# One hybrid decoder layer: transposed products gathered in one half bank of PSUM, with their evacuation and the SSD inputs' products on VectorE

## The chip, the cores and the metric

The kernel runs on one core of one Trainium2 chip. The metric is the device time of one execution in microseconds (us), lower is better. The median of three runs of the kernel before is 1099.75 us.

## The reference, cut to what matters

One decoder layer on 256 rows of width 2048, in float32. A combined input projection feeds a Mamba-2 SSD head group and a sparse-attention head group with its token indexer; one output projection maps both into the residual, and a squared-ReLU MLP of width 8192 follows.

```python
h = rmsnorm(x, g_mix) @ w_in
z, xbc, dt, q, k, v, qi, ki, wi = _split(h, IN_SIZES)
xbc = jax.nn.silu(causal_dwconv(xbc, conv_w, conv_b))
xs, bm, cm = _split(xbc, (SSD_WIDTH, N_BC, N_BC))
...
y = ssd_chunked(xs_f, dt_f, a, ...)          # uses xs * dt
y = y + d_skip.astype(jnp.float32)[:, None] * xs_f
...
y_att = dsa_attention(q, k, v, qi, ki, wi)   # scores from relu(qi . ki), top 64 keys
x = x + jnp.concatenate([y_ssd, y_att], axis=-1) @ w_out
u = rmsnorm(x, g_mlp) @ w_up
return x + jnp.square(jax.nn.relu(u)) @ w_down
```

## The kernel before, in words

Each matrix product is done with weights and activations split into a high and a low part, and three terms are summed: high by high, low by high, high by low. `operands` loads a weight tile on SP's queue (L122), ScalarE casts out the high part (L125) and VectorE subtracts it to get the low part (L126). It has 4 buffers for the raw tile (`raw`) and 5 for the split one (`w2`), and the splits are given high priority, so that they run ahead of TensorE.

There are two kinds of product. `product` has rows on partitions and sums all three terms in one whole bank for each of two row blocks (L148 to L150). `product_t` has columns on partitions: it makes 256 output columns by 256 rows from four weight tiles, with matmuls that stream 256 columns (L200). It is used for 4 blocks of the indexer's queries (`qi`), 6 blocks of the convolution's channels (`xbc`) and the 32 blocks of `w_up`, 42 in all. Before, it holds two banks, one for each 128 output columns; in each, the high by high term goes to the first half bank and the other two terms to the second half. `total` then adds the halves: ScalarE copies one half out of PSUM (L209), VectorE adds the other (L210).

The order of TensorE's instructions is that of the program. Small tasks (convolution, scores, top-k, SSD, attention) are Python generators; `step` advances them between groups of matmuls, so that their transposes and small matmuls are spread over the big products. The order on the other engines is set ahead of time by a planner from priorities and its own costs, and does not change when the chip runs.

For each `xbc` block, `conv` evacuates the product into `xraw` (L209, L210), GpSimd multiplies it by the rows' norm factors into `pad` (L510), ScalarE and VectorE do the four taps (L514, L516), and ScalarE the SiLU (L518). Blocks 0 to 3 are transposed by TensorE (L524), and ScalarE copies the result from PSUM to `xs` (L525). When the third block's task is done, `inputs` multiplies on GpSimd: `xs` by `dt` into `xdt` (in `room`, L535, two halves), `xdt` by the state's decay into `xdd` (L537), and `xs` by the skip weight in place (L540, two halves). Blocks 4 and 5 are the `bc` tile. The block `m1` of the input projection (608 columns in two K tiles, L148 to L150 with 304 columns) follows the `xbc` blocks in TensorE's order; inside it stand the small matmuls `ps_cb` (L550), which wait for `bc`. Beside them VectorE sums the indexer's scores (`sc`, L480) and takes the top 64 keys (L488, L489).

In the MLP, `up` evacuates each `w_up` product with `total`, squares its positive part on VectorE (L797), and splits the result again (L799, L800); `down` multiplies by `w_down`.

Of the kernel before, what the change touches and what calls it, by code (L numbers as in the profile page):

```python
# [9 lines left out]
F32 = mybir.dt.float32  # L10
F32R = mybir.dt.float32r
I32 = mybir.dt.int32
AF = mybir.ActivationFunctionType
OP = mybir.AluOpType
AX = mybir.AxisListType

P = 128
D = 2048
T = 256
NB = T // P  # L20
KT = D // P
# [47 lines left out]
def hymba_kernel(ctx: ExitStack, tc: tile.TileContext, xn, xt, w_in, w_out, w_up, w_down, vcol, vrow, out):  # L69
    nc = tc.nc  # L70
# [4 lines left out]
    ps = ctx.enter_context(tc.tile_pool(name="ps", bufs=4, space=bass.MemoryType.PSUM))  # L75
    mid_stack = ExitStack()
    mid = mid_stack.enter_context(tc.tile_pool(name="mid", bufs=1))

    u4 = dict(tag="u4", bufs=6)
    u2 = dict(tag="u2", bufs=6)  # L80
# [28 lines left out]
    def vcp(name, i=0):  # L109
        return vc[:, VC[name] + i:VC[name] + i + 1]  # L110
# [20 lines left out]
    def mp(name):  # L131
        other.append(name)
        return ps.tile([P, 512], F32, name=name, tag="mid")

    def accumulators():
        return [ps.tile([P, 512], F32, name="acc", tag="acc") for _ in range(2)]

    def product(src, n, left, load=None, tail=None):


        acc = accumulators()
        last = KT if tail is None else KT - 4

        def part(kt, out, b, wh, wl):
            s = slice(b * P, (b + 1) * P)
            ah, al = left(kt)
            free = tail is not None
            nc.tensor.matmul(out, ah[:, s], wh, start=(kt == 0), stop=False, skip_group_check=free)  # L148
            nc.tensor.matmul(out, al[:, s], wh, start=False, stop=False, skip_group_check=free)  # L149
            nc.tensor.matmul(out, ah[:, s], wl, start=False, stop=(kt == KT - 1), skip_group_check=free)  # L150

        kept = []
        halves = [slice(0, n // 2), slice(n // 2, n)]
        if tail is not None:
            acc.append(mp("acc_t"))
        for kt in range(KT):
            if kt % 2 == 0:
                hi, lo = operands(src[kt // 2], 2 * n, load, 0 if tail is None else SPARE - SHIFT_T)
            w = slice(kt % 2 * n, kt % 2 * n + n)
            wh, wl = hi[:, w], lo[:, w]  # L160
            if tail is None:
                for b in range(NB):
                    part(kt, acc[b][:, :n], b, wh, wl)
            elif kt < last:
                for c in halves if kt else [slice(0, n)]:
                    part(kt, acc[0][:, c], 0, wh[:, c], wl[:, c])
                for i, c in enumerate(halves):
                    part(kt, acc[1 + i][:, c], 1, wh[:, c], wl[:, c])
            else:
                kept.append((kt, wh, wl))  # L170
            step()
        if tail is not None:
            for kt, wh, wl in kept:
                for c in halves:
                    part(kt, acc[0][:, c], 0, wh[:, c], wl[:, c])
            tail(0, slice(0, n), acc[0])
            for i, c in enumerate(halves):
                for kt, wh, wl in kept:
                    part(kt, acc[1 + i][:, c], 1, wh[:, c], wl[:, c])
                tail(1, c, acc[1 + i][:, c])  # L180
        other.append("product")
        return acc

    def product_t(src, right):

        acc = accumulators()
        for i in range(4):
            hi, lo = operands(src[i], 1024, shift=SHIFT_T)
            c = i % 2
            for k in range(8):  # L190
                kt = 8 * (i // 2) + k
                x = right(kt)
                s = slice(k * P, (k + 1) * P)
                todo = [(hi, 0, 0, T), (lo, T, 0, T), (hi, T, T, T)]

                if other:
                    other.clear()
                    todo[:1] = [(hi, 0, 0, P), (hi, P, P, T - P)]
                for j, (w, at, fr, n) in enumerate(todo):
                    nc.tensor.matmul(acc[c][:, at:at + n], w[:, s], x[:, fr:fr + n], start=(kt + j == 0),  # L200
                                     stop=(kt == KT - 1 and j == len(todo) - 1), skip_group_check=True)
                if k % 4 == 3:
                    step()
        return acc

    def total(dst, acc):

        for c in range(2):
            nc.scalar.copy(dst[:, c, :], acc[c][:, T:])  # L209
            nc.vector.tensor_tensor(dst[:, c, :], acc[c][:, :T], dst[:, c, :], op=OP.add)  # L210


    ones = keep.tile([P, P], F32, name="ones")
# [3 lines left out]
    pt = ps.tile([P, 512], F32, name="ps_w", tag="mid")  # L217
# [40 lines left out]
    for name, cols in IN_BLOCKS:  # L258
        n = sum(b - a for a, b in cols)
# [47 lines left out]
    rrow = mid.tile([P, T], F32, name="rrow")  # L307
# [22 lines left out]
    xdt = room[:, :2048].rearrange("p (c x) -> p c x", c=NB)  # L330
# [73 lines left out]

    def index_queries(acc):

        t = mid.tile([P, 2, T], F32, name="qi", **u2)
        total(t, acc)
        st = mid.tile([P, 4, T], F32R, name="qis", **u4)
        qis.append(st)  # L410
        s4 = st.rearrange("p (c r) t -> p c r t", r=2)
        for i in range(2):
            s, o = slice(64 * i, 64 * i + 64), slice(64 - 64 * i, 128 - 64 * i)
            nc.scalar.copy(s4[s, :, i, :], t[s])
            nc.vector.tensor_tensor(s4[o, :, i, :], t[s], s4[s, :, i, :].bitcast(F32), op=OP.subtract)


    def row(n, w=16):
        return vr[:, VR[n]:VR[n] + w]

    dt = mid.tile([P, NB, 16], F32, name="dt")
# [3 lines left out]
    dst_ = mid.tile([P, 16], F32, name="dstate")  # L425
# [75 lines left out]
    xs = mid.tile([P, NB, 1024], F32, name="xs")  # L501
    bc = mid.tile([P, 4, T], F32, name="bc")
    hd = lambda t: t.rearrange("p (h d) -> p h d", d=64)

    def conv(acc, i):
        raw = mid.tile([P, 2, T], F32, name="xraw", **u2)
        total(raw, acc)
        pad = mid.tile([P, 2, T + 3], F32, name="pad", tag="pad", bufs=2)
        nc.gpsimd.memset(pad[:, :, :3], 0.0)
        nc.gpsimd.tensor_tensor(pad[:, :, 3:], raw, rrow[:, None, :].to_broadcast([P, 2, T]), op=OP.mult)  # L510
        o = mid.tile([P, 2, T], F32, name="xc", **u2) if i < 4 else bc[:, 2 * (i - 4):2 * (i - 4) + 2, :]
        for j in range(2):
            ct = 2 * i + j
            nc.scalar.activation(o[:, j, :], pad[:, j, 0:T], AF.Copy, scale=vcp("conv_w", ct))  # L514
            for k in range(1, 4):
                nc.vector.scalar_tensor_tensor(o[:, j, :], pad[:, j, k:k + T], vcp("conv_w", 12 * k + ct), o[:, j, :],  # L516
                                               op0=OP.mult, op1=OP.add)
            nc.scalar.activation(o[:, j, :], o[:, j, :], AF.Silu, bias=vcp("conv_b", ct))  # L518
        if i < 4:
            yield Y["conv"]  # L520
            pt = mp("ps_xs")
            for c in range(NB):
                for j in range(2):
                    nc.tensor.transpose(pt[:, (2 * c + j) * P:(2 * c + j + 1) * P], o[:, j, c * P:(c + 1) * P], ident)  # L524
            nc.scalar.copy(xs[:, :, 256 * i:256 * i + 256], pt.rearrange("p (c x) -> p c x", c=NB))  # L525

    xdd = [None]
    bn = mid.tile([P, T], F32, name="bn")
# [1 line left out]

    def inputs():
        yield "conv3"
        for c in range(NB):
            x3 = hd(xs[:, c, :])
            nc.gpsimd.tensor_tensor(hd(xdt[:, c, :]), x3, dt[:, c, :, None].to_broadcast([P, 16, 64]), op=OP.mult)  # L535
        xdd[0] = mid.tile([P, 1024], F32, name="xdd", **u4)
        nc.gpsimd.tensor_tensor(hd(xdd[0]), hd(xdt[:, 0, :]), dst_[:, :, None].to_broadcast([P, 16, 64]), op=OP.mult)  # L537
        for c in range(NB):
            x3 = hd(xs[:, c, :])
            nc.gpsimd.tensor_tensor(x3, x3, row("d_skip")[:, :, None].to_broadcast([P, 16, 64]), op=OP.mult)  # L540

    def states():
        yield "conv5"
# [233 lines left out]
    first = product_t(w_up[0], x2)  # L777
# [13 lines left out]
    def up(q):  # L791
        uh = mlp.tile([P, KT, T], F32R, name="uh")
        ul = mlp.tile([P, KT, T], F32R, name="ul")
        for j in range(8):
            r = mlp.tile([P, 2, T], F32, name="r")
            total(r, first if q + j == 0 else product_t(w_up[8 * q + j], x2))
            nc.vector.scalar_tensor_tensor(r, r, 0.0, r, op0=OP.max, op1=OP.mult)  # L797
            s = slice(2 * j, 2 * j + 2)
            nc.scalar.copy(uh[:, s, :], r)  # L799
            nc.vector.tensor_tensor(ul[:, s, :], r, uh[:, s, :].bitcast(F32), op=OP.subtract)  # L800
        return uh, ul
# [72 lines left out]
```

## Time and profile before

| | |
|---|---|
| median of 3 runs | 1099.75 us (1098.17 to 1099.8) |
| the profiled execution: time, span from the first to the last instruction | 1098.6 us, 1096.5 us |
| TensorE matmul busy | 1086.4 us, 99% of the span |
| TensorE weight load busy | 987.4 us, 90% |
| VectorE busy | 689.8 us, 63% |
| ScalarE busy | 534.5 us, 49% |
| GpSimd busy | 42.0 us, 4% |
| mean granted TensorE clock | 1.000 |

The time is about 2 us above the span, for what lies around the first and the last instruction. Shares of busy time are means over stages with different limits; matmuls are pipelined, and their ends are modelled, so that a busy TensorE can still be short of its pace.

### The profile page before, as it was taken

The numbers are of one execution on the slowest core, as the hardware profiler recorded it, in microseconds if no ns is written. First come the engines' busy times: TensorE is split into PE (matmuls) and PEld (weight loads), VectorE is DVE, ScalarE is ACT, GpSimd is POOL, SyncE is SP. The second block draws the span as 40 slices with busy tenths as digits, with TensorE's granted clock in tenths as the row PEclk, the third lists the DMA queues.
The fourth block names the chain that finished last, engine by engine and source line by source line (L and its number), as shares of the span: only waits on it lengthen the run. The fifth ranks groups of instructions, "written<-read, shape, count | busy, mean of one in ns | idle before, by whom it ended". The sixth has DMA issues, their size and how long they took to land.

```text
span 1096.5 us, 17759 instructions
## 1 busy us (share of the span) xinstructions
PE 1086.4 (99%) x7098; PEld 987.4 (90%) x7098; DVE 689.8 (63%) x976; ACT 534.5 (49%) x749; POOL 42.0 (4%) x41
## 2 busy tenths in 40 slices
PE   9999998999999999999999999999999999999998
PEld 7999997888888899999998889998889999888888
DVE  6776999677765666666665456665555665554443
ACT  7755555555765554444443334444334444333331
POOL 0010031122000000000000000000000000000000
PEclk9999999999999999999999999999999999999999
DMA  9856434643475556666566666665665666565662
GB/s 312 275 200 191 141 122 156 213 155 118 132 245 181 188 176 195 196 194 197 191 197 193 192 192 192 194 194 192 194 196 192 196 196 193 194 192 192 212 211 78
DMA packets 63746, 207.54 MB, mean 189 GB/s; under 512 B 7216, under 2 KB 11568, under 8 KB 63664
## 3 DMA queue, kind: packets, MB, share of 16 engines
q1 hardware_dynamic: 63520, 206.36, 58.8%
q8 instruction: 56, 0.92, 0.4%
q14 instruction: 26, 0.21, 0.1%
q10 hardware_dynamic: 144, 0.05, 0.0%
HBM read 204.29 MB, written 2.10 MB: 188 GB/s over the span
## 4 chain that ended last, share of the span: by engine, by line
PE 92%; DVE 3%; DMA 2%; issue 1%; ACT 1%; SPq 0%; ACTq 0%; DVEq 0%
PE acc L200 40%; PE acc L148 16%; PE acc L150 16%; PE acc L149 16%; DMA raw<-in_w_in 2%; DVE w L126 1%; DVE bc L516 1%; PE ps_y L587 1%; DMA xrow<-in_xn 1%; PE ps_sr L671 0%; PE ps_l L625 0%; PE ps_o L650 0%; ACT w L125 0%; PE ps_dec L578 0%; DVE sc L480 0%
## 5 line engine op out<-in xcount | busy, mean ns | idle before, releaser
L126 DVE TENSOR_TENSOR w<-raw,w 128x1024 fp32r<-128x1024 f32 (+3 forms) x400 | 468.5, 1174 | 374.1 <-ACT w L125 373.6
L125 ACT CAST w<-raw 128x1024 fp32r<-128x1024 f32 (+3 forms) x400 | 399.7, 1003 | 478.4 <-PE acc L150 255.5
L200 PE MATMUL acc<-x2x,w 128*128 128x256 f32 (+1 forms) x3077 | 349.8, 276 | 0.0
L200 PEld LDWEIGHTS acc<-x2x,w 128*128 128x128 f32 x3077 | 349.4, 188 | 0.2
L148 PE MATMUL acc<-w,uh 128*128 128x512 f32 (+1 forms) x527 | 199.9, 379 | 0.0
L149 PE MATMUL acc<-w,ul 128*128 128x512 f32 (+1 forms) x527 | 199.8, 379 | 0.0
L150 PE MATMUL acc<-w,uh 128*128 128x512 f32 (+1 forms) x527 | 199.8, 379 | 0.0
L150 PEld LDWEIGHTS acc<-w,uh 128*128 128x128 f32 x527 | 98.9, 188 | 18.8
L148 PEld LDWEIGHTS acc<-w,uh 128*128 128x128 f32 x527 | 98.9, 188 | 18.7
L149 PEld LDWEIGHTS acc<-w,ul 128*128 128x128 f32 x527 | 98.9, 188 | 18.7
L200 PE MATMUL acc<-hx,w 128*128 128x256 f32 (+1 forms) x978 | 114.9, 277 | 0.0
L200 PEld LDWEIGHTS acc<-hx,w 128*128 128x128 f32 x978 | 112.7, 188 | 0.0
L150 PE MATMUL acc<-w,hx 128*128 128x512 f32 (+1 forms) x224 | 82.6, 369 | 4.2 <-DVE w L126 4.1
L148 PE MATMUL acc<-w,hx 128*128 128x512 f32 (+1 forms) x224 | 85.0, 379 | 0.1
L149 PE MATMUL acc<-w,hx 128*128 128x512 f32 (+1 forms) x224 | 81.8, 365 | 0.0
L150 PEld LDWEIGHTS acc<-w,hx 128*128 128x128 f32 x224 | 42.0, 188 | 12.3 <-DVE w L126 5.8
L148 PEld LDWEIGHTS acc<-w,hx 128*128 128x128 f32 x224 | 42.2, 189 | 7.1 <-ACT w L125 0.8
L149 PEld LDWEIGHTS acc<-w,hx 128*128 128x128 f32 x224 | 42.1, 188 | 6.9 <-issue 0.7
L808 DVE SCALAR_TENSOR_TENSOR xr<-acc,rs,xr 128x512 f32<-128x512 f32 (+1 forms) x32 | 22.3, 735 | 9.2 <-PE acc L150 9.2
L210 DVE TENSOR_TENSOR r<-acc,r 128x256 f32<-128x256 f32 x64 | 26.8, 418 | 0.0
L148 PE MATMUL acc<-w,yah 128*128 128x512 f32 x64 | 25.7, 402 | 0.0
L148 PE MATMUL acc<-w,ysh 128*128 128x512 f32 x64 | 25.1, 392 | 0.0
(220 smaller groups left out, 726.7 us busy)
## 6 DMA issues: line engine op xcount, KB each, us to landing
raw<-in_w_up SPq DMA_DIRECT2D x128, 512.0 KB, 4.3
raw<-in_w_down SPq DMA_DIRECT2D x128, 512.0 KB, 4.4
raw<-in_w_in SPq DMA_DIRECT2D x72, 512.0 KB, 3.6
raw<-in_w_out SPq DMA_DIRECT2D x32, 512.0 KB, 3.5
raw<-in_w_in SPq DMA_DIRECT2D x16, 256.0 KB, 4.5
raw<-in_w_in SPq DMA_DIRECT2D x16, 152.0 KB, 5.3
raw<-in_w_in SPq DMA_DIRECT2D x8, 304.0 KB, 2.9
xT<-in_xt SPq DMA_DIRECT2D x16, 128.0 KB, 4.4
```

Source lines behind the costliest of these rows:

```text
L125: nc.scalar.copy(hi[:, s], raw[:, s])
L126: nc.vector.tensor_tensor(lo[:, s], raw[:, s], hi[:, s].bitcast(F32), op=OP.subtract)
L148: nc.tensor.matmul(out, ah[:, s], wh, start=(kt == 0), stop=False, skip_group_check=free)
L149: nc.tensor.matmul(out, al[:, s], wh, start=False, stop=False, skip_group_check=free)
L150: nc.tensor.matmul(out, ah[:, s], wl, start=False, stop=(kt == KT - 1), skip_group_check=free)
L200: nc.tensor.matmul(acc[c][:, at:at + n], w[:, s], x[:, fr:fr + n], start=(kt + j == 0), stop=(kt == KT - 1 and j == len(todo) - 1), skip_g ...
L210: nc.vector.tensor_tensor(dst[:, c, :], acc[c][:, :T], dst[:, c, :], op=OP.add)
L516: nc.vector.scalar_tensor_tensor(o[:, j, :], pad[:, j, k:k + T], vcp("conv_w", 12 * k + ct), o[:, j, :], op0=OP.mult, op1=OP.add)
L587: nc.tensor.matmul(pt[:, 64 * i:64 * i + 64], m[i // 4][:, i % 4, :], xdt[:, c, 64 * h:64 * h + 64], start=True, stop=True)
L808: nc.vector.scalar_tensor_tensor(xr[:, b, c], acc, rs4[:, b:b + 1], xr[:, b, c], op0=OP.mult, op1=OP.add)
```

## The change

`product_t` holds one bank in place of two: each 128 output columns have one half bank, in which all three terms are summed. `total` is gone. The consumers read the product from PSUM themselves: `index_queries` with the casts and subtractions that it had; `conv` with the multiplication into `pad`, which moves from GpSimd to VectorE; `up` with a ReLU on ScalarE and a multiplication by the product on VectorE. After the transposes in `conv`, VectorE multiplies the result from PSUM by the skip weight into `xs` and by `dt` into `xdt`, block by block, in place of ScalarE's copy and GpSimd's four multiplications over whole rows; `xdd` moves from GpSimd to VectorE.

```diff
-    def accumulators():
-        return [ps.tile([P, 512], F32, name="acc", tag="acc") for _ in range(2)]
+    def accumulator():
+        return ps.tile([P, 512], F32, name="acc", tag="acc")
     def product(src, n, left, load=None, tail=None):
-        acc = accumulators()
+        acc = [accumulator(), accumulator()]
     def product_t(src, right):
-        acc = accumulators()
+        acc = accumulator().rearrange("p (c t) -> p c t", c=2)
...
-                todo = [(hi, 0, 0, T), (lo, T, 0, T), (hi, T, T, T)]
+                todo = [(hi, 0, 0, T), (lo, 0, 0, T), (hi, 0, T, T)]
...
-                    nc.tensor.matmul(acc[c][:, at:at + n], w[:, s], x[:, fr:fr + n], start=(kt + j == 0),
-                                     stop=(kt == KT - 1 and j == len(todo) - 1), skip_group_check=True)
+                    nc.tensor.matmul(acc[:, c, at:at + n], w[:, s], x[:, fr:fr + n], start=(i + k + j == 0),
+                                     stop=(i >= 2 and k == 7 and j == len(todo) - 1), skip_group_check=True)
-    def total(dst, acc):
-        for c in range(2):
-            nc.scalar.copy(dst[:, c, :], acc[c][:, T:])
-            nc.vector.tensor_tensor(dst[:, c, :], acc[c][:, :T], dst[:, c, :], op=OP.add)
     def index_queries(acc):
-        t = mid.tile([P, 2, T], F32, name="qi", **u2)
-        total(t, acc)
...
-            nc.scalar.copy(s4[s, :, i, :], t[s])
-            nc.vector.tensor_tensor(s4[o, :, i, :], t[s], s4[s, :, i, :].bitcast(F32), op=OP.subtract)
+            nc.scalar.copy(s4[s, :, i, :], acc[s])
+            nc.vector.tensor_tensor(s4[o, :, i, :], acc[s], s4[s, :, i, :].bitcast(F32), op=OP.subtract)
     def conv(acc, i):
-        raw = mid.tile([P, 2, T], F32, name="xraw", **u2)
-        total(raw, acc)
...
-        nc.gpsimd.tensor_tensor(pad[:, :, 3:], raw, rrow[:, None, :].to_broadcast([P, 2, T]), op=OP.mult)
+        nc.vector.tensor_tensor(pad[:, :, 3:], acc, rrow[:, None, :].to_broadcast([P, 2, T]), op=OP.mult)
...
-            nc.scalar.copy(xs[:, :, 256 * i:256 * i + 256], pt.rearrange("p (c x) -> p c x", c=NB))
+            x4 = pt.rearrange("p (c h d) -> p c h d", c=NB, d=64)
+            for dst, f in ((xs, row("d_skip")[:, None, 4 * i:4 * i + 4, None]), (xdt, dt[:, :, 4 * i:4 * i + 4, None])):
+                nc.vector.tensor_tensor(dst[:, :, 256 * i:256 * i + 256].rearrange("p c (h d) -> p c h d", d=64), x4,
+                                        f.to_broadcast([P, NB, 4, 64]), op=OP.mult)
     def inputs():
         yield "conv3"
-        for c in range(NB):
-            x3 = hd(xs[:, c, :])
-            nc.gpsimd.tensor_tensor(hd(xdt[:, c, :]), x3, dt[:, c, :, None].to_broadcast([P, 16, 64]), op=OP.mult)
         xdd[0] = mid.tile([P, 1024], F32, name="xdd", **u4)
-        nc.gpsimd.tensor_tensor(hd(xdd[0]), hd(xdt[:, 0, :]), dst_[:, :, None].to_broadcast([P, 16, 64]), op=OP.mult)
-        for c in range(NB):
-            x3 = hd(xs[:, c, :])
-            nc.gpsimd.tensor_tensor(x3, x3, row("d_skip")[:, :, None].to_broadcast([P, 16, 64]), op=OP.mult)
+        nc.vector.tensor_tensor(hd(xdd[0]), hd(xdt[:, 0, :]), dst_[:, :, None].to_broadcast([P, 16, 64]), op=OP.mult)
     def up(q):
-            total(r, first if q + j == 0 else product_t(w_up[8 * q + j], x2))
-            nc.vector.scalar_tensor_tensor(r, r, 0.0, r, op0=OP.max, op1=OP.mult)
+            acc = first if q + j == 0 else product_t(w_up[8 * q + j], x2)
+            nc.scalar.activation(r, acc, AF.Relu)
+            nc.vector.tensor_tensor(r, r, acc, op=OP.mult)
```

## Rows read from the trace of the kernel before

**Rows 1.** The page's busy time: us, share of the span, instructions.

```profile
PE 1086.4 (99%) x7098; PEld 987.4 (90%) x7098; DVE 689.8 (63%) x976; ACT 534.5 (49%) x749; POOL 42.0 (4%) x41
```

**Rows 2.** The page's chain that ended last, shares of the span by engine.

```profile
PE 92%; DVE 3%; DMA 2%; issue 1%; ACT 1%; SPq 0%; ACTq 0%; DVEq 0%
```

**Rows 3.** Busy us (x instructions) by stretch: PE, PEld, DVE, ACT, POOL; PEclk, DMA, GB/s.

```profile
118.00:157.00 39.00, 39.00 (x344) 39.00 (x344) 36.67 (x77) 24.54 (x42) 5.51 (x7) 1.00 0.48 148
157.00:170.00 13.00, 13.00 (x109) 12.97 (x109) 11.80 (x11) 4.22 (x10) 10.94 (x5) 1.00 0.10 25
170.00:184.00 14.00, 9.37 (x61) 8.25 (x60) 13.55 (x35) 5.84 (x11) 1.29 (x1) 1.00 0.52 155
...
400.00:1093.00 693.00, 692.97 (x4671) 636.44 (x4668) 393.35 (x418) 298.44 (x349) 0.00 (x0) 1.00 0.60 191
```

**Rows 4.** Timeline of PE, block m1: start, us, instruction [idle before <- releaser].

```profile
165.75 0.30 PE L148 MATMUL acc<-w,hx 128*128 128x304 f32 x1
...
170.97 0.30 PE L149 MATMUL acc<-w,hx 128*128 128x304 f32 x1
...
174.01 0.41 PE L150 MATMUL acc<-w,hx 128*128 128x304 f32 x1 [2.74 <-DVE w L126]
...
176.88 0.41 PE L150 MATMUL acc<-w,hx 128*128 128x304 f32 x1 [0.93 <-DVE w L126]
...
183.58 0.94 PE L550 MATMUL ps_cb<-bc 128*128 128x128 f32 x6 [0.54 <-ACT bc L518]
...
186.25 0.39 PE L148 MATMUL acc<-w,hx 128*128 128x512 f32 x1
```

**Rows 5.** Timeline of POOL, 132 to 169 us.

```profile
132.59 1.29 POOL L510 TENSOR_TENSOR pad<-xraw,rrow 128x512 f32<-128x512 f32 x1 [7.75 <-DVE xraw L210]
...
157.68 4.80 POOL L535 TENSOR_TENSOR room<-xs,dt 128x1024 f32<-128x1024 f32 x2 [2.09 <-ACT xs L525]
162.44 2.08 POOL L537 TENSOR_TENSOR xdd<-room,dstate 128x1024 f32<-128x1024 f32 x1
164.49 4.13 POOL L540 TENSOR_TENSOR xs<-xs,vr 128x1024 f32<-128x1024 f32 x2
```

**Rows 6.** Timeline of DVE, 132 to 169 us.

```profile
132.63 2.33 DVE L126 TENSOR_TENSOR w<-raw,w 128x1024 fp32r<-128x1024 f32 x1
...
157.09 0.88 DVE L516 SCALAR_TENSOR_TENSOR bc<-pad,vc,bc 128x256 f32<-128x256 f32 x2
...
158.59 4.17 DVE L516 SCALAR_TENSOR_TENSOR bc<-pad,vc,bc 128x256 f32<-128x256 f32 x2
162.68 2.12 DVE L480 SCALAR_TENSOR_TENSOR sc<-rl,wis,sc 128x256 f32<-128x256 f32 x1
164.73 2.12 DVE L516 SCALAR_TENSOR_TENSOR bc<-pad,vc,bc 128x256 f32<-128x256 f32 x1
168.02 1.25 DVE L126 TENSOR_TENSOR w<-raw,w 128x608 fp32r<-128x608 f32 x1 [1.17 <-ACT w L125]
```

**Rows 7.** Timeline of ACT, the last SiLU of block 4.

```profile
166.89 0.51 ACT L518 ACTIVATE bc<-bc,vc 128x256 f32<-128x256 f32 x1 [5.63 <-DVE bc L516]
```

**Rows 8.** Groups by line and shape on DVE: count, busy us, mean ns, idle before.

```profile
L210 DVE TENSOR_TENSOR xraw<-acc,xraw 128x256 f32<-128x256 f32 x12 | 5.0, 416 | 0.0
...
L691 DVE TENSOR_TENSOR xs<-xs,zs 128x512 f32<-128x512 f32 x4 | 2.7, 684 | 0.8 <-ACT zs L687 0.8
...
L635 DVE TENSOR_TENSOR L<-L,sm 128x1024 f32<-128x1024 f32 x2 | 2.4, 1220 | 0.0
...
L595 DVE TENSOR_TENSOR yo<-ps_yo,eac 128x512 f32<-128x512 f32 x2 | 1.4, 686 | 0.1
```

**Rows 9.** Timeline of PE, end of the last product: first and last of 12 matmuls.

```profile
1090.09 0.28 PE L148 MATMUL acc<-w,uh 128*128 128x256 f32 x1
...
1091.34 0.28 PE L150 MATMUL acc<-w,uh 128*128 128x256 f32 x1
```

**Rows 10.** The chain in order of time: start, us, its longest piece.

```profile
400.23 170.12 PE acc L200 x1501
```

## The prediction

> **What bounds the kernel now.** I read the page's busy times and its chain of waits first. TensorE is busy for 1086.4 of 1096.5 us [rows 1] and makes 92% of the chain [rows 2], so time can only be won where TensorE waits, or lost where something delays it. Next come the sums by stretch, to find where it waits. [...] The one stretch with a hole in the middle of the run is 170 to 184 us, where TensorE is busy for 9.37 of 14 us and VectorE for 13.55 [rows 3].
>
> The timeline of TensorE shows that hole in block `m1`. It starts at 165.75 and ends where the next block begins, at 186.25, after 20.5 us [rows 4]. Its pace can be read ahead of the hole: 37 steps in the 5.22 us from 165.75 to 170.97, 0.141 us each. The block has 96 matmuls (16 K tiles, two row blocks, three terms), so 13.5 us; the small `ps_cb` matmuls and two transposes inside it take some 1.2 us (six of eight show 0.94). That leaves 20.5 - 13.5 - 1.2 = 5.8 us lost. Most of it waits for VectorE's split of the weights (2.74 and 0.93 us of idle time, and some shorter ones), the last bit for `bc` (0.54) [rows 4].
>
> Why is the split late? From 157.68 to 168.62 GpSimd does the five multiplications of `inputs` (4.80 + 2.08 + 4.13 us) [rows 5]. In just that time VectorE's instructions, which read two tensors from SBUF as GpSimd's do, stretch: two taps of `bc` take 4.17 us, where two took 0.88 right before it, and one score sum and one more tap take 2.12 us each [rows 6]. ScalarE, whose order is fixed, stands 5.63 us before the SiLU of that block [rows 7], with casts of weights queued behind it; VectorE then idles for 1.17 us for such a cast [rows 6]. When GpSimd is done, VectorE has scores, top-k and splits piled up, and TensorE runs dry at 171 us. In 157 to 170 us the DMA share is 0.10 [rows 3]: the raw tiles that are loaded are not released, so loading stops too.
>
> **The change part by part.** *The sum in one half bank.* The number of matmuls and their columns stay; three in a row now add to the same 256 columns. The last product already does this: at its end 12 matmuls in a row add 256 columns to one half bank, and their starts go from 1090.09 to 1091.34, 11 steps of 0.114 us [rows 9]. The `product_t` of now, which alternates halves, takes 170.12 / 1501 = 0.113 us [rows 10]. So I cost it at nothing, with bounds from nothing to 0.001 us on 42 x 96 = 4032 matmuls, 4 us at most, which is what the reading's last digit leaves.
>
> *Evacuation of `w_up` and `qi`.* Per block two copies on ScalarE and two additions on VectorE go. They lie under a full TensorE [rows 3], and so does the ReLU with its product in their place. Nothing won; if the cover were gone, it would be a gain, as there is less work than before. A `product_t` takes one of the four accumulator buffers and not two, and TensorE did not wait for these.
>
> *VectorE's ledger, 118 to 184 us and a little ahead of it.* Removed: 12 additions of 0.416 us, 5.0 us. Added: six multiplications into `pad` and eight into `xs` and `xdt`, all 128x512 with one input from PSUM. The nearest row is L595, the same form with the same kind of broadcast factor, 0.686 us; 14 x 0.686 = 9.6 us. `xdd` is 128x1024 from SBUF, as L635, 1.22 us [rows 8]. Net: 9.6 + 1.2 - 5.0 = +5.8 us of VectorE work.
>
> PSUM as a source costs nothing extra here: 0.686 us against 0.684 for the same shape from SBUF (L691) [rows 8]. [...]
>
> *What VectorE gets back.* In the stretch of `inputs`, 4.17 + 2.12 + 2.12 = 8.41 us for four instructions, which take 0.44 each otherwise (half of 0.88): 6.65 us [rows 6]. The idle 1.17 us goes with it: 7.8 us. During the pad multiplications of 1.29 us on GpSimd [rows 5] VectorE is held too: one split took 2.33 us [rows 6], where that size takes 1.22 [rows 8], 1.1 us lost. Six such give between 0 and 6.6 us; I take half, 3.3. Together 11.1 us, against +5.8: VectorE comes out 5.3 us ahead. Before 157 us it is about 1 us behind (eight additions go, -3.3; five pads and six products come, +7.5; relief, -2.7; so +1.5 at most), and VectorE has 39 - 36.67 = 2.3 us free there [rows 3]. From 157 us on it gains nearly all of the 7.8 us, which is more than the hole.
>
> *Latency and queues.* A block's path loses a copy, an addition, and a 1.29 us multiplication on GpSimd behind them; it gains one of 0.686 us. So `bc` is ready earlier, and the `ps_cb` wait should go as well. In the input stage ScalarE loses 20 copies (L209) and the four copies of `xs`, so its casts come no later. No DMA is added or moved; SP's loads wait on raw buffers, which come free earlier.
>
> **The sum.** Of 5.8 us lost I take 5.3 as won; 0.5 stays, since the orders on VectorE and ScalarE are fixed ahead and each short wait leaves a refill. On the profiled execution's own time that is 1098.6 - 5.3 = 1093.3 us. That execution was 1.15 us under the median of the runs (1099.75), so the prediction for the median is 1093.3 + 1.15 = 1094.4 us. After that TensorE is full through the rest of the input stage; what is late next, the loading before its products start and the writing of the result behind its last matmul, is not touched.
>
> **The rivals.** *Part of the hole stays* (chance 0.10 for about half, 0.10 for a loss of less than 2 us). VectorE is busy for 13.55 of 14 us in the hole [rows 3]; if its new order puts the eight top-k rounds or the score sums ahead of splits, TensorE still runs dry. For it: today's order does that. Against it: those splits were late because all ahead of them was. It gives 1098.6 - 2.9 + 1.15 = 1096.9 us with half won, 1098 to 1100 with nearly nothing.
>
> *Slower: VectorE becomes the bound* (0.06). If the stretched instructions were not GpSimd's doing, the +5.8 us comes with no relief. VectorE's free time in 118 to 184 us is 2.3 + 1.2 + 0.45 = 4.0 us [rows 3]; it decides from there, and between 1.8 and all 5.8 us would fall on TensorE: 1101.5 to 1105.5 us. The new products also wait on transposes at the head of VectorE's queue, with splits behind them. Against it: the stretch begins and ends with GpSimd's work, to within a microsecond [rows 5, 6].
>
> *Slower: the half bank* (0.01). If adding to the same columns cost more than the tail shows, each 0.001 us would cost 4 us, and from 0.0013 us on the gain would be gone. Rows 9 stand against it.
>
> **How the numbers follow.** The forecast has 0.73, with its own range 1093.1 to 1096.0 (all 5.8 us won, less 0.8 us for the runs' spread around their median, up to a residue of 2 us). About 0.2% of the time, 2.2 us, is what a measurement can tell from no change. Faster: 0.73 + 0.10 = 0.83; the same: 0.10; slower: 0.07. The range of 1092.6 to 1098.4 us takes in the half-won case and the runs' own spread, and leaves out the rest of the near-nothing case and the slower ones.
>
> **What would show it.** GpSimd idle between its early multiplications and those of the SSD part; taps (L516 of now) at 0.44 to 0.48 us throughout; block `m1` down from 20.5 to about 15 us; TensorE's pace in `product_t` still 0.113 us; the stretch after 400 us unchanged in length. The prediction is wrong if TensorE waits for splits at another place between 118 and 200 us, if the new VectorE instructions take clearly more than 0.69 us, or if the pace of 0.113 us moves.

## The result, and the profile after

The changed kernel takes 1092.78 us (median of 4 runs, 1092.03 to 1093.06), the kernel before 1099.78 us beside it (4 runs, 1098.17 to 1100.4): the ratio is 0.9938, with a 95% interval of 0.992 to 0.9955. It was forecast at 1094.4 us, in a range of 1092.6 to 1098.4, with a chance of 0.83 for faster. In a later comparison on one chip it took 1092.8 us (5 runs) against 1099.32 (9 runs), ratio 0.994 (0.9926 to 0.9954). Between the two profiled executions the span falls from 1096.5 to 1090.7 us, by 5.8 us.

The page's busy time and its chain by engine, after:

```profile
PE 1084.6 (99%) x7098; PEld 987.5 (91%) x7098; DVE 657.5 (60%) x907; ACT 526.6 (48%) x693; POOL 24.3 (2%) x30
...
PE 95%; DVE 2%; DMA 1%; ACT 1%; issue 1%; SPq 0%; ACTq 0%; DVEq 0%
```

TensorE has the same 7098 matmuls; VectorE has lost 32 us and GpSimd 18 us of work, and TensorE's share of the chain has risen from 92% [rows 2] to 95%. The sums by stretch say where (columns as in [rows 3]: PE, PEld, DVE, ACT and POOL busy, granted clock, DMA share, GB/s):

```profile
118.00:157.00 39.00, 39.00 (x344) 39.00 (x343) 37.54 (x82) 21.10 (x32) 0.31 (x3) 1.00 0.50 149
157.00:170.00 13.00, 13.00 (x109) 13.00 (x109) 12.55 (x28) 4.56 (x9) 0.00 (x0) 1.00 0.27 73
170.00:184.00 14.00, 14.00 (x95) 13.39 (x94) 13.82 (x31) 9.46 (x15) 0.00 (x0) 1.00 0.81 240
...
400.00:1088.00 688.00, 687.25 (x4620) 630.81 (x4618) 364.94 (x346) 293.46 (x312) 0.00 (x0) 1.00 0.61 191
```

From 170 to 184 us TensorE is busy for all of the 14 us, where it was for 9.37 [rows 3]. VectorE is as busy there as before (13.82 of 14 us), but it is in time. GpSimd does nothing. After 400 us VectorE has some 28 us less to do, and nothing comes of it, since TensorE was full there already (692.97 of 693 us [rows 3]; after, its last matmul ends shortly ahead of 1088 us). Block `m1` in TensorE's timeline, from its first matmul to the first of the next block:

```profile
166.03 0.30 PE L148 MATMUL acc<-w,hx 128*128 128x304 f32 x1
...
180.50 0.39 PE L148 MATMUL acc<-w,hx 128*128 128x512 f32 x1
```

It takes 14.47 us for 20.5 [rows 4], 6.0 us less, which is the whole difference of the spans. VectorE's timeline in the stretch in which GpSimd had its five multiplications (L472 are the score sums, L518 the products into `xs` and `xdt`, here `room`, L528 `xdd`):

```profile
157.68 0.68 DVE L518 TENSOR_TENSOR xs<-ps_xs,vr 128x512 f32<-128x512 f32 x1
158.28 0.78 DVE L126 TENSOR_TENSOR w<-raw,w 128x608 fp32r<-128x608 f32 x1
...
160.37 1.22 DVE L528 TENSOR_TENSOR xdd<-room,dstate 128x1024 f32<-128x1024 f32 x1
161.50 0.79 DVE L126 TENSOR_TENSOR w<-raw,w 128x608 fp32r<-128x608 f32 x1
162.21 2.11 DVE L472 SCALAR_TENSOR_TENSOR sc<-rl,wis,sc 128x256 f32<-128x256 f32 x4
```

Four score sums take 2.11 us together, where one alone took 2.12 [rows 6], and a split of 608 columns 0.78 us. The groups of the new and of the relieved instructions, from 40 to 200 us (L500 is `pad`, L506 are the taps):

```profile
L506 DVE SCALAR_TENSOR_TENSOR bc<-pad,vc,bc 128x256 f32<-128x256 f32 x12 | 5.1, 480 | 0.0
L500 DVE TENSOR_TENSOR pad<-acc,rrow 128x512 f32<-128x512 f32 x6 | 4.1, 686 | 0.4 <-PE acc L200 0.4
...
L518 DVE TENSOR_TENSOR xs<-ps_xs,vr 128x512 f32<-128x512 f32 x4 | 2.7, 685 | 0.0
L518 DVE TENSOR_TENSOR room<-ps_xs,dt 128x512 f32<-128x512 f32 x4 | 2.7, 684 | 0.0
```

The last reading is the pace of `product_t`. The chain's longest piece is the same 1501 matmuls in the same time as in [rows 10], now three in a row into one half bank. With the last evacuation behind it:

```profile
394.51 170.12 PE acc L200 x1501
...
1087.29 0.48 DVE xr L797
```

In the kernel before the same evacuation stands here:

```profile
1093.01 0.48 DVE xr L808
```

From the one row to the other it is 692.78 us in both kernels, so the stretch after 400 us has kept its length.

### The profile page after: what moved, and what is told of

The parts are those of the page before. It is cut to its first block, busy times and chain, and to the rows that moved or that the text cites. A ratio compares the mean times of both kernels' runs of the same rounds, so it can differ in the third digit from the quotient of the medians.

```text
span 1090.7 us, 17557 instructions
## 1 busy us (share of the span) xinstructions
PE 1084.6 (99%) x7098; PEld 987.5 (91%) x7098; DVE 657.5 (60%) x907; ACT 526.6 (48%) x693; POOL 24.3 (2%) x30
## 4 chain that ended last, share of the span: by engine, by line
PE 95%; DVE 2%; DMA 1%; ACT 1%; issue 1%; SPq 0%; ACTq 0%; DVEq 0%
PE acc L200 41%; PE acc L148 16%; PE acc L150 16%; PE acc L149 16%; DVE w L126 1%; PE ps_y L575 1%; DMA xrow<-in_xn 1%; PE ps_sr L659 0%; PE ps_l L613 0%; PE ps_o L638 0%; DMA raw<-in_w_in 0%; ACT xrow L245 0%; DMA xT<-in_xt 0%; PE ps_s L465 0%; PE ps_s L466 0%
## 5 line engine op out<-in xcount | busy, mean ns | idle before, releaser
L148 PE MATMUL acc<-w,yah 128*128 128x512 f32 x64 | 25.7, 402 | 0.0
L150 PE MATMUL acc<-w,yah 128*128 128x512 f32 x64 | 25.0, 391 | 0.0
```

## The experiments

The theory: GpSimd's five multiplications, which read SBUF, hold VectorE's instructions that read two tensors from SBUF (beside them two taps took 4.17 us, where two took 0.88 right before [rows 6]); VectorE's splits come late, and TensorE waits for them in `m1`. Rivals: the half bank with its lighter evacuation won the time; the shorter path of the pads won it; or VectorE's own work, not GpSimd's, made it late. "Block" below is the time of `m1` read as above.

**The half bank alone.** The changed kernel with both groups of multiplications given back to GpSimd.

```diff
+        raw = mid.tile([P, 2, T], F32, name="xraw", **u2)
+        nc.scalar.copy(raw, acc)
-        nc.vector.tensor_tensor(pad[:, :, 3:], acc, rrow[:, None, :].to_broadcast([P, 2, T]), op=OP.mult)
+        nc.gpsimd.tensor_tensor(pad[:, :, 3:], raw, rrow[:, None, :].to_broadcast([P, 2, T]), op=OP.mult)
...
+            nc.scalar.copy(xs[:, :, 256 * i:256 * i + 256], pt.rearrange("p (c x) -> p c x", c=NB))
     # and `inputs` as it was, with its five multiplications on GpSimd
```

> The half bank and the evacuation without the moves to VectorE: products sum in one half bank, queries and the MLP read PSUM, but the pad multiplications (from a ScalarE copy) and the five multiplications of the inputs are GpSimd's again, as before. Theory (GpSimd's block of multiplications made VectorE late): the hole in block m1 stays, 20 to 21 us for the block where the changed kernel takes 14.5, and the time is that of before within 2 us, 1098 to 1101 us. Rival (the lighter evacuation or the half bank won the time): the block takes about 15 us, time 1093 to 1094 us.

1100.02 us (11 runs), 1.0006 of the kernel before (0.9997 to 1.0014); the block takes 21.3 us. The half bank and the lighter evacuation, with all of the MLP part, bring nothing, and the 1501 matmuls take 170.12 us here too. The hole is there again, in TensorE's timeline:

```profile
176.32 0.41 PE L150 MATMUL acc<-w,hx 128*128 128x304 f32 x1 [3.57 <-DVE w L126]
...
179.32 0.62 PE L150 MATMUL acc<-w,hx 128*128 128x304 f32 x1 [0.45 <-DVE w L126]
```

**Only the inputs given back.** The second half of the edit above alone.

> The changed kernel with one part undone: ScalarE copies xs from PSUM and GpSimd does the five multiplications of the inputs again; the pad multiplications stay on VectorE. Theory: VectorE's taps and score sums beside GpSimd's block stretch to 2.1 us each again, TensorE loses 4 to 6 us in block m1, time 1097 to 1099 us. Rival (the pads' shorter path won it): 1 us or less lost, 1093 to 1094 us.

1096.74 us (8 runs), 0.9974 (0.9964 to 0.9985): 4.0 us of the changed kernel's gain are lost, a little less than expected, and the block takes 17.9 us. VectorE's timeline beside GpSimd's block, which runs from 159.61 to 170.44 us:

```profile
160.04 2.12 DVE L472 SCALAR_TENSOR_TENSOR sc<-rl,wis,sc 128x256 f32<-128x256 f32 x1
162.09 2.49 DVE L126 TENSOR_TENSOR w<-raw,w 128x608 fp32r<-128x608 f32 x1
164.51 6.74 DVE L472 SCALAR_TENSOR_TENSOR sc<-rl,wis,sc 128x256 f32<-128x256 f32 x4
```

The four score sums that took 2.11 us take 6.74. This run and the one before differ in the pads alone and were taken on one chip: with the pads on VectorE it is 3.3 us faster, and the block 3.4 us shorter. So the pads do count as long as GpSimd has the five multiplications. Whether that is VectorE's relief or the shorter path to `bc` was not tried.

**Only the pads given back.** The first half of that edit alone.

> The changed kernel with the other part undone: the pad multiplications on GpSimd again, from a ScalarE copy out of PSUM; the inputs' products stay on VectorE. Theory: each pad holds VectorE for about 1 us, but VectorE has that much room, so at most 1 us is lost, 1092.5 to 1094 us. Rival (the pads' path won it): block m1 takes 18 us or more, 1096 to 1099 us.

1093.35 us (5 runs), 0.9943 (0.9931 to 0.9955), 0.6 us above the changed kernel, and the block takes 14.5 us as after. Once the five multiplications are off GpSimd, the pads win nothing that can be measured.

**Only the inputs moved.** The kernel before with one word changed in three places; two banks, `total` and the pads on GpSimd stay.

```diff
-            nc.gpsimd.tensor_tensor(hd(xdt[:, c, :]), x3, dt[:, c, :, None].to_broadcast([P, 16, 64]), op=OP.mult)
+            nc.vector.tensor_tensor(hd(xdt[:, c, :]), x3, dt[:, c, :, None].to_broadcast([P, 16, 64]), op=OP.mult)
     # the same for xdd and for xs by d_skip
```

> The kernel before with only the five multiplications of the inputs moved to VectorE, whole rows from SBUF, 1.22 us each. Theory: VectorE gets 6.1 us of work and sheds about 7.8 us of stretched instructions and waits, so most of the hole closes: 2 to 5 us won, 1094.5 to 1097.5 us; the rest of the change's gain is in reading PSUM directly. Rival (the gain needs the half bank and the lighter evacuation): no gain or a loss, 1099 to 1104 us.

1093.48 us (5 runs), 0.9943 (0.993 to 0.9955). The direction was right, the size too small: 5.6 us are won against the 1099.03 us of the kernel before beside it, where the changed kernel won 7.0 and 6.5, and the block takes 14.75 us, 0.28 us more than after. So reading PSUM directly has no share in the gain that these runs can show. VectorE does the five multiplications in 1.2 us each, between splits that come in time:

```profile
159.27 2.35 DVE L535 TENSOR_TENSOR room<-xs,dt 128x1024 f32<-128x1024 f32 x2
161.54 0.78 DVE L126 TENSOR_TENSOR w<-raw,w 128x608 fp32r<-128x608 f32 x1
162.24 1.21 DVE L537 TENSOR_TENSOR xdd<-room,dstate 128x1024 f32<-128x1024 f32 x1
163.38 2.35 DVE L540 TENSOR_TENSOR xs<-xs,vr 128x1024 f32<-128x1024 f32 x2
165.65 0.78 DVE L126 TENSOR_TENSOR w<-raw,w 128x608 fp32r<-128x608 f32 x1
```

**GpSimd's reads, with nobody waiting for them.** The changed kernel plus five multiplications whose results go into space that is overwritten later.

```diff
+        scr = yah[:, :4, :].rearrange("p k t -> p (k t)")
+        for n in range(5):
+            nc.gpsimd.tensor_tensor(hd(scr), hd(xs[:, n % 2, :]), dt[:, n % 2, :, None].to_broadcast([P, 16, 64]), op=OP.mult)
         nc.vector.tensor_tensor(hd(xdd[0]), ...)
```

> The changed kernel, complete, plus five multiplications 128x1024 on GpSimd at the place of the old inputs' block, which read xs and dt from SBUF into space that is overwritten later; nobody waits for them, and the orders of all other engines are the same. Theory (GpSimd's reads hold VectorE's instructions with two inputs from SBUF): VectorE's score sums, splits and taps in that stretch go to 1.2 to 2.1 us, TensorE waits again for 2 to 6 us in block m1, 1095 to 1099 us. Rival (VectorE's and ScalarE's own work or the waits on GpSimd's results made the hole): no change, 1092 to 1093.5 us.

1099.6 us (11 runs), 1.0 of the kernel before (0.9991 to 1.0009), 0.6 us above the expected band: the whole gain is gone, though nothing waits for GpSimd, and VectorE and ScalarE have the changed kernel's work in the changed kernel's order. The block takes 21.7 us. The wait in TensorE's timeline, then GpSimd's block:

```profile
174.27 0.41 PE L150 MATMUL acc<-w,hx 128*128 128x304 f32 x1 [3.32 <-DVE w L126]
```

```profile
157.91 11.73 POOL L530 TENSOR_TENSOR yah<-xs,dt 128x1024 fp32r<-128x1024 f32 x5 [13.29 <-DVE xs L518]
```

VectorE's timeline beside it (L531 is `xdd`):

```profile
158.45 2.13 DVE L472 SCALAR_TENSOR_TENSOR sc<-rl,wis,sc 128x256 f32<-128x256 f32 x1
160.50 0.68 DVE L518 TENSOR_TENSOR room<-ps_xs,dt 128x512 f32<-128x512 f32 x1
161.10 1.52 DVE L472 SCALAR_TENSOR_TENSOR sc<-rl,wis,sc 128x256 f32<-128x256 f32 x1
162.54 2.92 DVE L531 TENSOR_TENSOR xdd<-room,dstate 128x1024 f32<-128x1024 f32 x1
165.39 2.49 DVE L126 TENSOR_TENSOR w<-raw,w 128x608 fp32r<-128x608 f32 x1
```

All of these with two inputs from SBUF are stretched: 0.48 to 2.13 and 1.52 us, 1.22 to 2.92, 0.78 to 2.49. The product in between, with one input from PSUM, takes its 0.68 us beside GpSimd.

**GpSimd's writes.** In the place of those multiplications, zeros into a tile that is written later, 18 times, behind one small product that fixes the place.

```diff
+        nc.gpsimd.tensor_tensor(cbm[:, 0, 0, :64], xs[:, 0, 960:], xs[:, 1, 960:], op=OP.mult)
+        for n in range(18):
+            nc.gpsimd.memset(cbm, 0.0)
         nc.vector.tensor_tensor(hd(xdd[0]), ...)
```

> As the run with GpSimd's added reads, but GpSimd fills a tile 128x512 with zeros 18 times, about 10 us of work that only writes. If only reads hold VectorE: no stretched instruction, 1092 to 1093.5 us. If any work of GpSimd holds it: the same stretch and the same loss as with the reads.

1094.14 us (5 runs, 1092.52 to 1094.69), 0.9947 (0.9935 to 0.9959); the block takes 14.5 us. GpSimd's timeline, then VectorE's beside it:

```profile
160.74 10.48 POOL L530 MEMSET cbm<- 128x512 f32 x18
```

```profile
161.48 0.47 DVE L472 SCALAR_TENSOR_TENSOR sc<-rl,wis,sc 128x256 f32<-128x256 f32 x1
161.88 1.22 DVE L531 TENSOR_TENSOR xdd<-room,dstate 128x1024 f32<-128x1024 f32 x1
163.01 0.78 DVE L126 TENSOR_TENSOR w<-raw,w 128x608 fp32r<-128x608 f32 x1
163.71 2.11 DVE L472 SCALAR_TENSOR_TENSOR sc<-rl,wis,sc 128x256 f32<-128x256 f32 x4
```

GpSimd is busy for 10.5 us in the same place, and nothing is stretched. (The fills are also shorter than the multiplications, 0.58 us each for some 2.35; length by itself was not varied.) The median is slightly above the expected band; in this execution `m1` begins at 167.47 us for 166.03, so the time went ahead of `m1`, as it does from run to run (below).

**VectorE's own work.** The five added multiplications on VectorE in place of GpSimd.

```diff
-            nc.gpsimd.tensor_tensor(hd(scr), hd(xs[:, n % 2, :]), ...)
+            nc.vector.tensor_tensor(hd(scr), hd(xs[:, n % 2, :]), ...)
```

> The changed kernel plus the same five added multiplications 128x1024 on VectorE in place of GpSimd: 6.1 us more of VectorE's own work in the stretch in which it is busy for some 26 of 27 us. Theory (VectorE's lateness is what TensorE waits for, and top-k can move behind the splits): 0 to 4 us lost, 1093 to 1097 us, and less than with the reads on GpSimd. If VectorE is now the bound there, all of it shows: 1098 to 1099 us.

1094.97 us (5 runs), 0.9963 (0.995 to 0.9975): 6.1 us of added work on a nearly full engine (26.4 of 27 us busy from 157 to 184 us in the changed kernel) cost 2.2 us, where GpSimd's multiplications cost 6.8. The splits are not late; the planner has put the top-k rounds behind them. What is late is `bc`, for which TensorE waits once, and the block takes 16.6 us:

```profile
180.16 0.94 PE L541 MATMUL ps_cb<-bc 128*128 128x128 f32 x6 [1.85 <-ACT bc L508]
```

**The next wait.** With the hole gone, the longest wait left in TensorE's timeline of the changed kernel, after the loading at the start, stands before the transposes of the indexer's keys:

```profile
54.04 0.65 PE L391 MATMUL ps_ki<-ident,kd 128*128 128x128 f32 x2 [1.04 <-DVE kd L386]
```

```diff
-        yield 7
+        yield 12
         pt = mp("ps_ki")
```

> The changed kernel with the two transposes of the indexer's keys five steps later in TensorE's order (yield 12 for 7). In the trace of the changed kernel TensorE waits there for 1.2 us, with 0.3 us of refill. If nothing else is late: 1.2 to 1.5 us won, 1091.3 to 1091.6 us. Rival: the wait moves to the next small matmul behind it, 1092.8 us.

1091.55 us (5 runs, 1090.97 to 1091.71), 0.9926 (0.9913 to 0.9938), 1.2 us below the changed kernel, as expected. The two were not run on one chip, and the intervals of their ratios overlap; the next pair was run on one.

**The changed kernel again, and the two edits that count, alone.** The second run is the kernel before with only the five multiplications on VectorE and the later transposes.

> The changed kernel as it is, beside the next run on the same chip. 1092 to 1093.5 us; the median of more runs shows whether the 7.0 us between the first medians hold, or rather the 5.8 us between the two profiled spans.

> The kernel before with two edits: the five multiplications of the inputs on VectorE (whole rows from SBUF), and the indexer's transposes five steps later. If GpSimd's block was the whole cause and the wait for the keys the last one left, this does as well as the changed kernel with its later keys: 1091 to 1092.5 us. If the half bank and the direct reads of PSUM bring something of their own, it stays at 1093 us or above.

On one chip: the changed kernel 1092.8 us (5 runs), 0.994 (0.9926 to 0.9954); the two edits on the kernel before 1090.89 us (5 runs, 1090.62 to 1091.22), 0.9919 (0.9906 to 0.9933). The latter is faster than both kernels, with the old two banks, the old evacuation and the old pads; its slowest run lies below the changed kernel's fastest (1092.0). The transposes no longer wait (no idle time in their row):

```profile
59.80 0.38 PE L397 MATMUL ps_ki<-ident,kd 128*128 128x128 f32 x2
```

## Why the prediction was right, step by step

**The place.** Right. The hole in `m1` was the one thing in reach. It was sized at 5.8 us lost; the block gave back 6.0. The 0.5 us kept for fixed orders and refills did not stay, and that is the error of the sum that the profiles show: 5.3 forecast, 5.8 between the spans. None of the three signs of being wrong came: TensorE's timeline has no wait from 118 to 200 us, the new products from PSUM take 0.69 us, and the pace stays.

**The rest of the distance to the median.** The median came out 1.6 us under the forecast; the 0.5 us above are one part of that. The other is the step from the profiled execution to the median (+1.15 us): it carried the first three runs' spread with it, and the changed kernel's own profiled execution lies on its median. So 1092.78 us is below the forecast case's own range (1093.1 to 1096.0 us) and only 0.2 us inside the whole range: that the number lies inside is in part luck, while the mechanism is not. The medians differ by 7.0 us at first, by 6.5 in the later pair. Runs differ ahead of the changed place: `m1` begins at 165.50, 166.03 and 167.47 us in three kernels in which VectorE and ScalarE have the same order, and the difference is there already at a fill of `pad` on GpSimd well ahead of it (122.55, 123.08 and 124.52 us). Why was not tried.

**The cause.** Right, and now shown from both sides. GpSimd's reads, with nobody waiting for their results, bring the hole back (the block takes 21.7 us); about the same time of writes does not (14.5 us); moving the five multiplications alone closes it (14.75 us). The two runs with added work also show which of VectorE's instructions are held: with two inputs from SBUF, a score sum takes 2.13 us for 0.48 beside GpSimd's reads and 0.47 beside its writes; the product with one input from PSUM takes its 0.68 us beside the reads. By what mechanism the reads hold them is not shown.

**VectorE's ledger.** The costs were right: 0.684 to 0.686 us for the products from PSUM and 1.22 for `xdd`. The relief of 7.8 us in the stretch of `inputs` carried the result. The 3.3 us of relief at the pads were real on VectorE: the instructions stretched beside the six pad multiplications in the kernel before add up to some 3.7 us. Their worth hangs on the other part: at most 0.6 us of time once the five multiplications are gone, 3.3 us while GpSimd has them.

**The half bank.** Costed at nothing, and nothing it is: 170.12 us for 1501 matmuls before, after, and with the half bank alone. The MLP's lighter evacuation is hidden whole, as stated.

**The rivals.** That part of the hole stays did not happen. That VectorE becomes the bound did not either, though the run with 6.1 us of work added to it shows how near it is: 2.2 us fall on TensorE, at `bc` and not at the splits.

## What to carry to other kernels

When an engine that is not the bottleneck is late in one stage, compare its instructions there with the same shapes elsewhere: here a time of 2.1 us for 0.44 came from another engine's work beside it, and taking that work away cured it, even though it gave the late engine more to do (+5.8 us of instructions, for 5.8 us won). To show such a cause, add the suspected work with nobody waiting for it, and then another form of work of about the same length in its place: here GpSimd's reads stretched a score sum to 2.13 us, and its writes left one at 0.47. And when a large diff wins time in one place, run its parts, in more than one combination: here one word edited in three places holds the gain as far as the runs can tell, and the pads are worth 3.3 us or nothing, by what stands beside them.

## What the runs showed of the hardware that was not expected

In the run with GpSimd's reads TensorE's granted clock dropped behind the wait, to 0.50, and the hole cost more than the waits in it. TensorE waits 3.32 us, and soon after, from 175.56 to 182.14 us, it starts a matmul of 304 columns every 0.25 us for 0.14. The sums by stretch (columns as in [rows 3]):

```profile
170.00:174.00 4.00, 0.95 (x7) 0.71 (x6) 3.72 (x10) 0.00 (x0) 0.00 (x0) 1.00 0.03 12
174.00:178.00 4.00, 3.10 (x14) 2.73 (x15) 3.90 (x11) 1.25 (x3) 0.00 (x0) 0.68 0.26 78
178.00:182.00 4.00, 4.00 (x18) 4.00 (x17) 4.00 (x9) 2.75 (x6) 0.00 (x0) 0.50 0.75 227
182.00:186.00 4.00, 4.00 (x32) 4.00 (x31) 3.90 (x11) 2.21 (x3) 0.00 (x0) 0.97 0.85 288
```

The clock is 0.50 from 178 to 182 us and 0.97 from 182 to 186, and at the end of the block the matmuls start every 0.14 us again; in the profile of the kernel before, with a wait of 2.74 us [rows 4], it stayed at 1.00 [rows 3].

The slow stretch costs time of its own. TensorE's timeline, then VectorE's next two splits:

```profile
177.41 0.62 PE L150 MATMUL acc<-w,hx 128*128 128x304 f32 x1 [0.63 <-DVE w L126]
...
180.62 0.46 PE L150 MATMUL acc<-w,hx 128*128 128x304 f32 x1
```

```profile
178.50 0.79 DVE L126 TENSOR_TENSOR w<-raw,w 128x608 fp32r<-128x608 f32 x1
...
179.99 0.79 DVE L126 TENSOR_TENSOR w<-raw,w 128x608 fp32r<-128x608 f32 x1
```

Up to the wait at 177.41 us a slow TensorE only waits less for its split. From there to 182.14 us it starts 18 more matmuls with no wait, while the next two splits, needed after 12 matmuls each, end at 179.29 and 180.78 us. At a step of 0.14 us, with a short wait for the first of these splits, it would reach the same matmul some 1.8 us sooner, an estimate from these rows. So of the 7.2 us by which the block is longer than in the changed kernel some 1.8 are the clock's, and the rest come from VectorE's lateness. The mean granted clock is below 1.0 in all 11 runs of this kernel and in all 11 of the half bank alone (0.996 to 0.998).

For the kernel before, the runs show no such cost. Its mean granted clock lies between 0.996 and 1.0, and the times of both kinds lie across each other (1097.64 to 1100.72 us at 1.0 and 1098.39 to 1101.78 below it in one set of 15).
